# Preparing the queries of the next attention tile one unit ahead, with two sets of query operands

## The chip, the cores and the metric

The kernel runs on one core of a Trainium2 chip. The core has five engines that each work through a queue of their own: TensorE (PE, matrix products and transposes), VectorE (DVE), ScalarE (ACT), GpSimd (POOL) and SyncE (SP), which here issues the transfers. The metric is device time in microseconds of one launch; less is better. Span means the time from the first to the last instruction in one profiled execution.

## The reference

One decoder layer on x of 1024 tokens by 1024 channels, in fp32. Three mixers run side by side on a normed input and a second part is a feed-forward network (FFN):

```
h = rmsnorm(x);  u_pool, q, kv, gates, B, C, X = split(h @ w_in)
y_pool = (window means of 2, 4, 8, 16 tokens - u_pool) @ pool_w * pool_scale    # 256 channels, 4 groups
y_attn = g0 * compressed + g1 * selected + g2 * window                          # 8 heads of 64, 2 key/value groups
y_conv = B * causal_dwconv3(C * X)                                              # 256 channels
x = x + concat(y_pool, y_attn, y_conv) @ w_out
h = rmsnorm(x);  a, g = split(h @ ffn_up)
x = x + (silu(causal_dwconv3(a)) * g) @ ffn_down                                # 2816 hidden units
```

The attention has three branches for each query. The compressed branch looks at 63 compressed keys (blocks of 32 tokens, stride 16). Its probabilities, added up by blocks of 64 tokens, choose the 8 blocks that the selected branch looks at. The window branch looks at the last 512 tokens. Each branch is a softmax with a linear bias by distance and a gate.

## The kernel before

Every fp32 product that needs its precision is made of three products of two parts: an operand is split into `hi` (L88 or L476, ACT) and the rest `lo` (L89 or L477, POOL or DVE), and hi·hi, hi·lo and lo·hi are added up in PSUM.

The program text only states the work. A list scheduler with a simulated timeline sets the order of the instructions on each engine, taking as priority the order in which the text emits them; so an instruction that the text emits later may stand earlier on its engine, and a changed order of emission moves much else. Buffers are rings: a tile with a tag waits until the ring's oldest holder was read for the last time.

The stages, in order of the text:
- First norm, products with `w_in`, compressed keys and values, queries. The queries go to DRAM (`qd`).
- Attention of tiles 0 to 3 of 128 tokens (`attend`, L639), and beside it, as filling work through two PSUM banks (`fill`), the short convolution and the two pooling halves (`pool_half`). A pooling half is: products of normed rows with 128 columns of `w_in` for two halves of the tokens (L211 to L213), copies to `hb` tiles (L694), window sums by doubling on DVE (L712), the scaling and subtraction on DVE (L719 to L721; the first half of the tokens has edge columns of its own), a product with the block-diagonal matrix `bdw` (L723), and a scaled copy on ACT (L725) that goes to DRAM.
- Attention of tiles 4 to 7, and beside it: the output product of the pooling and convolution channels for all tiles (`project`, L820 to L823), then for tiles 0 to 3 the output product of the attention channels, the second norm (`second_norm`: L171 scales, L97 flips, L180 and L181 split into `h2a`), all `up` products of the FFN for these tokens (L841 to L843), and the first three pairs of chunks of the second FFN product for them (L916 and L917; their hidden units, read back from DRAM, are split into `yh` and `yl`, two buffers each). At its end stands the output product of tiles 4 to 7.
- The rest of the FFN (L960), with PE alone to set the pace.

The attention of one tile i is four units: for the two groups g, the window branch (br 1) and the selected one (br 0). A unit has `scores`: per head products into S (L572, L573, masks L576 and L578), maximum (L580, DVE), exponential (L583, ACT), reciprocal (L586, DVE) and gating (L588, POOL). The `values` of the unit before are woven between: transposes of the probabilities (L97), their split (`pth` L476 ACT, `ptl` L477 DVE), products with the values (L609, L610), and after the selected branch the sum of two halves into `yf` (L621).

Ahead of its units a tile needs two functions. `prepare(i)` loads the queries `qn`, transposes them and makes the two operands `qA` (ring) and `qB` (fixed buffers `qB[g][i % QBUF]`, whose constant rows are written once). `compressed(i)` makes the compressed scores (L508 to L510), their softmax in `pc` (L512 maximum, L514 subtraction, L515 exponential, L517 sum, L519 reciprocal, L522 product), for tiles 4 to 7 the choice of blocks (L529 to L541, ending in `pen`, whose transpose goes to rows 96 to 111 of qB), the gating of pc (L549, POOL) and the transposes and split of pc that the values of the first unit read.

With QBUF = 1 the operands of tile i+1 overwrite those of tile i, and `attend` emits `prepare(i+1)` and `compressed(i+1)` after the last unit's scores:

```
            if u and u[1:] == (1, 0) and u[0] < tiles[-1]:
                prepare(u[0] + 1)
                compressed(u[0] + 1)
```

It starts with both for its first tile, so for tile 0 and again for tile 4.

Of the kernel before, what the change touches and what calls it, by code (L numbers as in the profile page):

```python
# [11 lines left out]
I32 = mybir.dt.int32  # L12
# [18 lines left out]
QBUF = 1  # L31

# columns of w_in
# [12 lines left out]
def kernel(  # L46
# [15 lines left out]
    # ------------------------------------------------------------------ pools  # L62
# [11 lines left out]
    def small(w, tag="s8", parts=P, bufs=None):  # L74
        return sm.tile([parts, w], F32, tag=tag, bufs=bufs, name=nm(tag))
# [10 lines left out]
    def split(hi, lo, src, lo_eng):  # L86
        """src = hi + lo exactly, both of at most 12 significant bits"""
        act.activation(hi, src, AF.Copy)  # L88
        lo_eng.tensor_tensor(lo, src, hi.bitcast(F32), ALU.subtract)  # L89

    # -------------------------------------------------------------- constants
# [3 lines left out]
    def flip(out, src, n=P):  # L95
        """transpose of n rows"""
        pe.transpose(out, src, ident[:n, :n])  # L97
# [3 lines left out]
    # rows laid on partitions by one transpose: ffn_conv 66, sconv 6, pool_scale 2, cmp_pos 32  # L101
# [3 lines left out]
    # DRAM scratch  # L105
# [3 lines left out]
    # x with the products of the mixers, then of the attention too  # L109
# [3 lines left out]
    # long-lived attention operands  # L113
# [11 lines left out]
    # values of the compressed branch: rows of the other group are zero  # L125
# [3 lines left out]
    # ---------------------------------------------------------- phase 1 setup  # L129
    pht = ExitStack()  # L130
    hp = pht.enter_context(tc.tile_pool(name="ht", bufs=1, side="right"))
    # normed rows, transposed: two halves of the tokens, each in two parts
# [24 lines left out]
    def rstd_of(ssq, width, n, parts=P, pre=""):  # L157
        """(ssq / n + eps) ** -0.5"""
# [6 lines left out]
    def norm_transpose(xt, g_bc, dst_hi, dst_lo, i, new, bank, pre=""):  # L165
        """RMSNorm of rows xt, transposed and split into dst[:, :, tile i]"""
# [16 lines left out]
    # ------------------------------------------------------------ w_in chunks  # L183
    def load_w(c0, lo_engs, gates=None):
        """256 columns of w_in, and 12 of its gate columns"""
# [11 lines left out]
    def load_w2(src, c0, c1, lo_engs):  # L197
        """two blocks of 128 columns"""
# [7 lines left out]
    def mm_ct(ps, wh, wl, sub, hv):  # L206
        """[channel, token] product of 128 columns with 512 tokens"""
# [7 lines left out]
    def mm_tc(ps, wh, wl, i, n=256):  # L215
        """[token, column] product of tile i with n columns"""
# [7 lines left out]
    def put_gates(ps, i, j):  # L224
        """sigmoid of 12 gate columns"""
# [6 lines left out]
    def head_norm(src, nh, gain, dst, parts=P):  # L232
        """RMSNorm over the 64 columns of each of nh heads; src in PSUM"""
# [11 lines left out]
    def put_v(src, i, br):  # L245
        """split the values [token, 2 groups x 64] of tile i into vv"""
# [5 lines left out]
    # ------------------------------------- first norm, keys and values (selected)  # L252
# [763 lines left out]
```

## Time and profile before

| | |
|---|---|
| Time, three runs | 1353.71, 1354.81 and 1356.84 us; median 1354.81 |
| Profiled execution | span 1351.4 us; what lies around the span is 3.4 us if this execution took the median |
| Busy, share of the span | PE 97%, DVE 56%, ACT 40%, POOL 37% |
| Granted clock of PE | 0.991 in the mean |

The page cuts the span into 40 slices of 33.8 us and gives the busy share in tenths, and the granted clock of PE in the same way:

```profile
PE   6999999999998999999999999999999999999998
...
PEclk9999998989998999999999999999999999999999
```

The slices with an 8 in one of the two rows stand at 203 to 236, 270 to 304 and 405 to 439 us, beside the first slice (start of the program) and the last. The windows in the section on the rows lie around them. In a window's row each engine has its busy time and, in brackets, its number of instructions; PEclk is the granted clock, 1.00 being full. An engine's idle time in a timeline stands in square brackets, with the instruction that ended it.

### The profile page before, as it was taken

How to read it: one execution, taken by the hardware profiler on the slowest of the kernel's cores; microseconds unless marked ns; L12 is line 12 of the kernel's file. 1: busy time of each engine (PE TensorE's matmuls, PEld its weight loads, DVE VectorE, ACT ScalarE, POOL GpSimd, SP SyncE). 2: the span in 40 equal slices, each digit the busy share in tenths (PEclk: the TensorE clock that was granted, in tenths of full speed). 3: DMA queues.
4: the chain of work that ended last, by engine and by line, in shares of the span. 5: the costliest groups of instructions: out<-in, count | busy, mean ns of one | idle time of the engine just before them, and what ended most of it. 6: DMA issues, size and time to landing. Idle time of an engine off the chain costs nothing.

```text
span 1351.4 us, 17763 instructions
## 1 busy us (share of the span) xinstructions
PE 1316.0 (97%) x6670; PEld 1083.8 (80%) x6670; DVE 752.6 (56%) x1351; ACT 536.6 (40%) x972; POOL 496.1 (37%) x447
## 2 busy tenths in 40 slices
PE   6999999999998999999999999999999999999998
PEld 5999987867776788888888878788888888888886
DVE  6762555566677545545654657674454555454554
ACT  5441433445355545444544454452312322132220
POOL 3453722242142544345443454353313331242220
PEclk9999998989998999999999999999999999999999
DMA  9011320145432322222222344231212422243221
GB/s 272 25 42 55 99 75 25 48 147 157 148 125 86 117 87 86 78 87 79 85 89 75 102 136 177 94 120 57 88 59 82 125 63 78 78 156 92 89 70 62
DMA packets 142498, 128.93 MB, mean 95 GB/s; under 512 B 10595, under 2 KB 119373, under 8 KB 142413
## 3 DMA queue, kind: packets, MB, share of 16 engines
q1 hardware_dynamic: 142269, 127.71, 29.9%
q8 instruction: 52, 0.85, 0.3%
q14 instruction: 33, 0.27, 0.1%
q10 hardware_dynamic: 144, 0.10, 0.0%
HBM read 105.50 MB, written 22.28 MB: 95 GB/s over the span
## 4 chain that ended last, share of the span: by engine, by line
PE 88%; DVE 5%; ACT 2%; DMA 2%; issue 1%; POOL 0%; SPq 0%; ACTq 0%; DVEq 0%
PE dn L960 13%; PE fill L841 9%; PE fill L843 9%; PE fill L842 9%; PE tr L97 5%; PE upg L841 3%; PE upg L843 3%; PE upg L842 3%; PE fill L916 3%; PE S L572 2%; PE fill L211 2%; PE fill L213 2%; PE fill L212 2%; PE S L573 2%; PE acc L609 2%; PE acc L610 2%
## 5 line engine op out<-in xcount | busy, mean ns | idle before, releaser
L89 POOL TENSOR_TENSOR wlo<-wst,whi 128x1024 fp32r<-128x1024 f32 x109 | 266.1, 2458 | 282.5 <-ACT whi L88 281.8
L588 POOL TENSOR_SCALAR pb<-pb,rc,gat 128x640 f32<-128x640 f32 (+7 forms) x128 | 105.9, 829 | 315.2 <-DVE rc L586 290.2
L88 ACT ACTIVATE whi<-wst 128x1024 fp32r<-128x1024 f32 x124 | 127.1, 1055 | 116.7 <-DMA wst<-in_ffn_up_dram 76.9
L963 DVE TENSOR_TENSOR x<-dn,x 128x1024 f32<-128x1024 f32 x72 | 88.0, 1222 | 103.8 <-PE dn L960 103.4
L841 PE MATMUL fill<-h2a_hi,whi 128*128 128x512 f32 x352 | 141.8, 403 | 0.5 <-DVE h2a_lo L181 0.5
L843 PE MATMUL fill<-h2a_hi,wlo 128*128 128x512 f32 x352 | 141.6, 402 | 0.0
L842 PE MATMUL fill<-h2a_lo,whi 128*128 128x512 f32 x352 | 141.6, 402 | 0.0
L583 ACT ACTIVATE pb<-S,mx 128x640 f32<-128x640 f32 (+7 forms) x128 | 89.6, 701 | 122.8 <-DVE mx L580 113.6
L477 DVE TENSOR_TENSOR ptl<-tr,pth 128x512 fp32r<-128x512 f32 x140 | 94.3, 686 | 64.7 <-ACT pth L476 32.7
L580 DVE TENSOR_REDUCE mx<-S 128x1 f32<-128x640 f32 (+7 forms) x128 | 89.6, 703 | 67.0 <-PE S L578 65.8
L476 ACT ACTIVATE pth<-tr 128x512 fp32r<-128x512 f32 x140 | 80.4, 596 | 79.1 <-PE tr L97 45.8
L960 PE MATMUL dn<-dl,hh 128*128 128x512 f32 x288 | 89.1, 390 | 0.0
L960 PE MATMUL dn<-dh,hh 128*128 128x512 f32 x288 | 88.6, 391 | 0.3 <-DVE x L963 0.3
L960 PE MATMUL dn<-dh,hl 128*128 128x512 f32 x288 | 88.8, 390 | 0.0
L97 PE MATMUL tr<-ident,pb 128*128 128x128 f32 x528 | 86.0, 276 | 1.1 <-POOL pb L588 1.1
L97 PEld LDWEIGHTS tr<-ident,pb 128*128 128x128 f32 x528 | 65.6, 142 | 15.1 <-POOL pb L588 1.6
L841 PEld LDWEIGHTS fill<-h2a_hi,whi 128*128 128x128 f32 x352 | 66.4, 189 | 14.1 <-DVE h2a_lo L181 0.8
L842 PEld LDWEIGHTS fill<-h2a_lo,whi 128*128 128x128 f32 x352 | 66.4, 189 | 13.5
L843 PEld LDWEIGHTS fill<-h2a_hi,wlo 128*128 128x128 f32 x352 | 66.3, 188 | 13.5
L848 DVE SCALAR_TENSOR_TENSOR f2k<-fill,colw,f2k 128x511 f32<-128x511 f32 x44 | 32.9, 748 | 79.3 <-ACT f2k L847 78.7
L572 PE MATMUL S<-blk,qA 128*128 128x320 f32 (+5 forms) x192 | 71.2, 371 | 5.8 <-ACT pb L583 5.7
L841 PE MATMUL upg<-h2b_hi,whi 128*128 128x512 f32 x176 | 69.2, 394 | 1.8 <-ACT whi L88 1.8
(275 smaller groups left out, 3123.2 us busy)
## 6 DMA issues: line engine op xcount, KB each, us to landing
wst<-in_ffn_up_dram SPq DMA_DIRECT2D x88, 512.0 KB, 3.7
wst<-in_ffn_down_dram SPq DMA_DIRECT2D x28, 512.0 KB, 3.6
wst<-in_w_in_dram SPq DMA_DIRECT2D x18, 512.0 KB, 4.5
wst<-in_w_out_dram SPq DMA_DIRECT2D x12, 512.0 KB, 3.9
hid<-f2k SPq DMA_DIRECT2D x22, 256.0 KB, 2.0
f2k<-hid SPq DMA_DIRECT2D x22, 256.0 KB, 4.2
b<-in_x_dram SPq DMA_DIRECT2D x8, 512.0 KB, 7.2
f<-in_x_dram SPq DMA_DIRECT2D x8, 512.0 KB, 3.4
```

The lines of the kernel that those rows point to most:

```text
L88: act.activation(hi, src, AF.Copy)
L89: lo_eng.tensor_tensor(lo, src, hi.bitcast(F32), ALU.subtract)
L97: pe.transpose(out, src, ident[:n, :n])
L477: dve.tensor_tensor(lo, pt, hi.bitcast(F32), ALU.subtract)
L572: pe.matmul(S[:, c, :cw], qAs[i, g][:, hh, :], kA[br, g][:, cols], start=True, stop=False)
L580: dve.tensor_reduce(mx, S[:, 0:nck, :cw], axis=AX.XY, op=ALU.max, negate=True)
L583: act.activation(pb[:, : ns * P].rearrange("p (c n) -> p c n", c=nck), S[:, 0:nck, :cw], AF.Exp, bias=mx, accum_out=sw)
L588: pool.tensor_scalar(pb[:, : ns * P], pb[:, : ns * P], rc, gat[:, i, col : col + 1], ALU.mult, ALU.mult)
L841: pe.matmul(ps, wh[:, kt, cols], h2[0][:, kt, :], start=kt == 0, stop=False)
L842: pe.matmul(ps, wh[:, kt, cols], h2[1][:, kt, :], start=False, stop=False)
L843: pe.matmul(ps, wl[:, kt, cols], h2[0][:, kt, :], start=False, stop=kt == KT - 1)
L960: pe.matmul(ps[:, nh - turn[0], :], h[:, tt], w[:, nh * 512 : nh * 512 + 512], start=k == 0 and h is hh and w is dh, stop=k == n - 1 and h ...
```

## The change

QBUF becomes 2: a second pair of qB buffers and two buffers for qA of each group. `compressed` is cut in two; `compressed_out` has the gating and the transposes of pc. `attend` emits the three for tile i+1 after three different units of tile i: `prepare` after the scores of (i, 0, 0), `compressed` after those of (i, 1, 1), `compressed_out` after those of (i, 1, 0). This holds across the border from tile 3 to tile 4 too, and only tile 0 has them at the front.

The second set takes room, so that other rings shrink: `qn` and `pc` share one buffer, `yb` moves into the ring of `pth`, `f2k` has 4 buffers instead of 5, `pg` 1 instead of 2, and five tags of small tiles 2 instead of 4. Comments and document strings are taken out too. Lines after the change have numbers 2 to 13 higher.

```diff
-QBUF = 1
+QBUF = 2
...
     def small(w, tag="s8", parts=P, bufs=None):
+        if tag in ("ssq4", "ms4", "rs4", "gate", "cbias"):
+            bufs = 2
...
-    auxq_i = at2.tile([P, P], I32, tag="qn", name="auxq_i")
-    auxq = at2.tile([P, P], F32, tag="qn", name="auxq")
+    auxq_i = at2.tile([P, P], I32, tag="pth", name="auxq_i")
+    auxq = at2.tile([P, P], F32, tag="qn", bufs=1, name="auxq")
...
-        qn = at2.tile([P, 512], F32, tag="qn", name=nm("qn"))
+        qn = at2.tile([P, 512], F32, tag="qn", bufs=1, name=nm("qn"))
...
-        pc = at2.tile([P, 8, 64], F32, tag="pc", bufs=1, name=nm("pc"))
+        pc = at2.tile([P, 8, 64], F32, tag="qn", bufs=1, name=nm("pc"))
...
-                pg = small(64, "pg", bufs=2)
+                pg = small(64, "pg", bufs=1)
...
+        pcg[i] = pc
+
+    def compressed_out(i):
+
+        pc = pcg[i]
         pc4 = pc.rearrange("p (h g) n -> p g h n", g=2)
...
-        yb = at2.tile([64, 4, P], F32, tag="yb", bufs=1, name=nm("yb"))
+        yb = at2.tile([P, 4, P], F32, tag="pth", name=nm("yb"))[0:64]
...
     def attend(tiles):
-        prepare(tiles[0])
-        compressed(tiles[0])
+        if tiles[0] == 0:
+            prepare(0)
+            compressed(0)
+            compressed_out(0)
...
-            if u and u[1:] == (1, 0) and u[0] < tiles[-1]:
-                prepare(u[0] + 1)
-                compressed(u[0] + 1)
+
+            if u and u[0] < NT - 1:
+                if u[1:] == (0, 0):
+                    prepare(u[0] + 1)
+                elif u[1:] == (1, 1):
+                    compressed(u[0] + 1)
+                elif u[1:] == (1, 0):
+                    compressed_out(u[0] + 1)
             prev = (u, pbs)
...
-        return f2.tile([P, 512], dt, tag="f2k", bufs=5, name=nm("f2k"))
+        return f2.tile([P, 512], dt, tag="f2k", bufs=4, name=nm("f2k"))
```

The scheduler's order then differs on every engine from the attention on. Three places follow, each before and after; in the rows a name has its buffer's number behind it.

DVE around the first pooling half, before: the last window sum, the last scaled sums and what comes behind them (`mx` with `tr` is the maximum of the compressed branch of tile 1).

```order
L712 TENSOR_TENSOR hb_3952<-hb_3950 64x525
L721 SCALAR_TENSOR_TENSOR hb_3932<-hb_3950,inv_w,hb_3932 64x512
L586 RECIPROCAL rc_470_2521<-sw_469_2519 128x1
L721 SCALAR_TENSOR_TENSOR hb_3932<-hb_3952,inv_w,hb_3932 64x512
L512 TENSOR_REDUCE mx_454_2479<-tr_2461 128x8
L580 TENSOR_REDUCE mx_472_2528<-S_2524 128x1
L580 TENSOR_REDUCE mx_480_2551<-S_2547 128x1
L514 TENSOR_TENSOR pc_2481<-tr_2461,mx_454_2479 128x512
L517 TENSOR_REDUCE sw_456_2484<-pc_2481 128x8
L519 RECIPROCAL rc_457_2486<-sw_456_2484 128x8
L522 TENSOR_TENSOR pc_2481<-pc_2481,rc_457_2486 128x512
```

DVE there after the change: the start of the same half, from the compressed maximum to the compressed sum.

```order
L514 TENSOR_REDUCE mx_430_2429<-tr_2411 128x8
L586 TENSOR_REDUCE mx_423_2398<-S_2394 128x1
L516 TENSOR_TENSOR pc_2431<-tr_2411,mx_430_2429 128x512
L725 TENSOR_TENSOR hb_4041<-hb_4010 128x527
L592 RECIPROCAL rc_426_2403<-sw_425_2401 128x1
L586 TENSOR_REDUCE mx_435_2443<-S_2439 128x1
L586 TENSOR_REDUCE mx_440_2455<-S_2451 128x1
L725 TENSOR_TENSOR hb_4043<-hb_4041 64x525
L732 TENSOR_TENSOR hb_4041<-hb_4041,inv_c 64x16
L734 SCALAR_TENSOR_TENSOR hb_4010<-hb_4041,inv_w,hb_4010 64x496
L519 TENSOR_REDUCE sw_432_2434<-pc_2431 128x8
```

The compressed branch has moved from behind the half to ahead of it and into it; its reciprocal and product (L521, L524) follow further on, before the second window sums.

DVE at the start of the second pooling half, before: the maximum of a head, then four window sums in a row.

```order
L580 TENSOR_REDUCE mx_602_2908<-S_2904 128x1
L712 TENSOR_TENSOR hb_4197<-hb_4166 128x527
L712 TENSOR_TENSOR hb_4199<-hb_4197 128x525
L712 TENSOR_TENSOR hb_4201<-hb_4199 128x521
L712 TENSOR_TENSOR hb_4203<-hb_4201 64x513
L719 TENSOR_TENSOR hb_4201<-hb_4201,inv_c 64x16
L721 SCALAR_TENSOR_TENSOR hb_4166<-hb_4201,inv_w,hb_4166 64x496
L477 TENSOR_TENSOR ptl_2843<-tr_2837,pth_2842 128x512
L719 TENSOR_TENSOR hb_4203<-hb_4203,inv_c 64x16
```

DVE there after the change, from the first window sum on.

```order
L725 TENSOR_TENSOR hb_4303<-hb_4272 128x527
L479 TENSOR_TENSOR ptl_3103<-tr_3097,pth_3102 128x512
L725 TENSOR_TENSOR hb_4305<-hb_4303 128x525
L725 TENSOR_TENSOR hb_4307<-hb_4305 128x521
L514 TENSOR_REDUCE mx_674_3143<-tr_3125 128x8
L725 TENSOR_TENSOR hb_4309<-hb_4307 64x513
L732 TENSOR_TENSOR hb_4307<-hb_4307,inv_c 64x16
L734 SCALAR_TENSOR_TENSOR hb_4272<-hb_4307,inv_w,hb_4272 64x496
L586 TENSOR_REDUCE mx_679_3157<-S_3153 128x1
L516 TENSOR_TENSOR pc_3145<-tr_3125,mx_674_3143 128x512
L586 TENSOR_REDUCE mx_685_3172<-S_3168 128x1
```

The compressed branch of tile 3 stands between the window sums and scalings now; its sum, reciprocal and product follow some ten rows on.

PE near the end of the early second FFN product, before: a few products L916 with attention work among them (`acc` are the value products of tile 7).

```order
L916 MATMUL fill_8915<-whi_8837,yh_8839 128x512
L916 MATMUL fill_8915<-wlo_8838,yh_8839 128x512
L609 MATMUL acc_6436<-pth_6480,vv 128x512
L916 MATMUL fill_8915<-whi_8837,yl_8840 128x512
L916 MATMUL fill_8915<-whi_8837,yh_8849 128x512
L916 MATMUL fill_8915<-wlo_8838,yh_8849 128x512
L916 MATMUL fill_8915<-whi_8837,yl_8850 128x512
L610 MATMUL acc_6436<-ptl_6481,vv 128x512
L609 MATMUL acc_6436<-pth_6505,vv 128x512
L97 MATMUL tr_6536<-ident,pb_6430 128x128
```

PE after the change, at the border of the second and the third pair of chunks: the next pair has other buffers of `yh` and of the weights.

```order
L929 MATMUL fill_8927<-whi_8849,yl_8852 128x512
L929 MATMUL fill_8927<-whi_8849,yh_8861 128x512
L929 MATMUL fill_8927<-wlo_8850,yh_8861 128x512
L929 MATMUL fill_8927<-whi_8849,yl_8862 128x512
L616 MATMUL acc_6448<-ptl_6620,vv 128x512
L615 MATMUL acc_6448<-pth_6630,vv 128x512
L616 MATMUL acc_6448<-ptl_6631,vv 128x512
L929 MATMUL fill_8957<-whi_8935,yh_8937 128x512
L929 MATMUL fill_8957<-wlo_8936,yh_8937 128x512
```

Three value products stand at this border, and at the one before it three transposes; from the third pair's end to the output product of tiles 4 to 7 no other work is left in the order.

## Rows read from the trace of the kernel before

**Rows 1.** The page: span and instructions, then busy time of each engine.
```profile
span 1351.4 us, 17763 instructions
...
PE 1316.0 (97%) x6670; PEld 1083.8 (80%) x6670; DVE 752.6 (56%) x1351; ACT 536.6 (40%) x972; POOL 496.1 (37%) x447
```

**Rows 2.** Windows: stretch, its length, busy time of each engine, granted clock, DMA.
```profile
193.00:214.88 21.88, 21.88 (x122) 18.35 (x120) 8.08 (x26) 7.97 (x27) 4.73 (x11) 1.00 0.14 44
214.88:227.83 12.95, 10.87 (x49) 8.12 (x47) 10.97 (x29) 5.47 (x17) 4.76 (x7) 0.69 0.08 20
...
290.60:312.20 21.60, 16.86 (x79) 11.03 (x77) 17.29 (x35) 13.94 (x31) 10.17 (x9) 0.84 0.63 218
...
390.97:397.94 6.97, 5.61 (x30) 3.60 (x28) 5.72 (x13) 5.82 (x14) 3.36 (x4) 1.00 0.64 212
397.94:447.37 49.43, 43.16 (x234) 34.75 (x233) 34.91 (x78) 28.00 (x56) 18.33 (x17) 0.93 0.27 91
447.37:800.00 352.63, 352.63 (x1781) 286.77 (x1782) 187.66 (x370) 166.58 (x288) 152.88 (x98) 1.00 0.28 86
```

**Rows 3.** List of waits of PE: total us, times, longest.
```profile
PE S L572 <- ACT pb L583: 5.7, 6, 2.1
...
PE fill L916 <- DVE x L917: 0.6, 1, 0.6
```

**Rows 4.** Timeline of DVE, first pooling half: start us, us, engine, line, operation.
```profile
219.73 0.42 DVE L499 TENSOR_TENSOR qA<-tr,qA 64x256 fp32r<-64x256 f32 x1
...
221.10 0.42 DVE L580 TENSOR_REDUCE mx<-S 128x1 f32<-128x256 f32 x1 [0.41 <-PE S L578]
...
225.93 0.75 DVE L721 SCALAR_TENSOR_TENSOR hb<-hb,inv_w,hb 64x512 f32<-64x512 f32 x1
226.72 0.69 DVE L512 TENSOR_REDUCE mx<-tr 128x8 f32<-128x512 f32 x1
```

**Rows 5.** Timeline of all engines, second pooling half.
```profile
287.27 2.91 DVE L712 TENSOR_TENSOR hb<-hb 128x527 f32<-128x527 f32 x4
...
290.21 0.17 DVE L719 TENSOR_TENSOR hb<-hb,inv_c 64x16 f32<-64x16 f32 x1
...
291.70 4.67 POOL L89 TENSOR_TENSOR wlo<-wst,whi 128x1024 fp32r<-128x1024 f32 x2 [4.29 <-ACT whi L88]
...
293.57 0.69 DVE L477 TENSOR_TENSOR ptl<-tr,pth 128x512 fp32r<-128x512 f32 x1 [2.56 <-ACT pth L476]
...
294.30 2.11 DVE L719 TENSOR_TENSOR hb<-hb,inv_c 64x16 f32<-64x16 f32 x1
...
300.73 0.16 DVE L586 RECIPROCAL rc<-sw 128x1 f32<-128x1 f32 x1 [0.75 <-ACT pb L583]
...
302.20 0.56 DVE L580 TENSOR_REDUCE mx<-S 128x1 f32<-128x384 f32 x1 [0.71 <-PE S L578]
...
303.29 0.84 DVE L621 TENSOR_TENSOR yf<-acc,yb 64x256 f32<-64x256 f32 x2
```

**Rows 6.** Timeline of PE: flips of normed rows, first product of the FFN.
```profile
397.94 1.10 PE L97 MATMUL fill<-ident,f 128*128 128x128 f32 x8
...
411.15 1.09 PE L97 MATMUL fill<-ident,f 128*128 128x128 f32 x8 [0.70 <-DVE f L171]
...
429.95 1.74 PE L97 MATMUL fill<-ident,f 128*128 128x128 f32 x8
...
445.36 1.04 PE L97 MATMUL fill<-ident,f 128*128 128x128 f32 x8
...
447.37 0.50 PE L841 MATMUL fill<-h2a_hi,whi 128*128 128x512 f32 x1 [0.53 <-DVE h2a_lo L181]
```

**Rows 7.** Chain of waits, a piece of products at full clock.
```profile
905.82 2.99 PE dn L960 x13
```

**Rows 8.** Operations on the tile yh: durations in ns, shortest, median, longest.
```profile
L88 ACT ACTIVATE yh<-f2k x21: 619/632/634, 308.6 to 870.9; 128x512 fp32r<-128x512 f32 x21
...
L89 POOL TENSOR_TENSOR yl<-f2k,yh x10: 1285/1298/1307, 371.4 to 848.2; 128x512 fp32r<-128x512 f32 x10
```

More of the change, by code (lines that the diff above doesn't have):

```diff
@@ L478, in put_pt @@
         return hi, lo
-    qAs, pcs, yfs, pos = {}, {}, {}, {}
+    qAs, pcs, pcg, yfs, pos = {}, {}, {}, {}, {}
     new_s, new_p = [None], [None]
     def prepare(i):
-        qn = at2.tile([P, 512], F32, tag="qn", name=nm("qn"))
+        qn = at2.tile([P, 512], F32, tag="qn", bufs=1, name=nm("qn"))
         nc.sync.dma_start(qn, qd[i])
```

## The prediction

> **What bounds the kernel now.** I read the page first. Its sum of busy times shows TensorE (PE) busy for 1316.0 of 1351.4 us, every other engine at 56% or less [rows 1]. So a change of order can win only what PE does not use: pauses, and stretches in which its clock is low. The windows come second, laid along the attention, because the change touches nothing after it but buffer counts. They show that this loss stands in few places [rows 2]. In the 352.63 us from 447.37 to 800.00, which hold most of the boundaries between tiles 4 to 7, PE works 352.63 us at full clock: preparing the next tile later or earlier is worth nothing there. From 193.00 to 214.88 it is the same, 21.88 of 21.88 us. The loss stands in four windows: the second part of the first pooling half (214.88 to 227.83, pause 12.95 − 10.87 = 2.08 us, clock 0.69), that of the second (290.60 to 312.20, 4.74 us, 0.84), the run-up to the second norm (390.97 to 397.94, 1.36 us) and the second norm of tiles 0 to 3 (397.94 to 447.37, 6.27 us, 0.93). The pauses add up to 14.45 us; the low clock costs at most 12.95 × 0.31 + 21.60 × 0.16 + 49.43 × 0.07 = 10.9 us. All that could be won is 25.4 us at the most.
>
> The list of waits comes third. PE's own waits for the attention's softmax chain are small, S behind the previous head's exponential 5.7 us in six [rows 3], so the waits the change aims at are short. What VectorE (DVE) has queued in the four windows decides, and I read its timeline there.
>
> **First pooling half.** The DVE work of this half (L712 to L721) fills the window from its start to 226.68, mixed with softmax work of tiles 0 and 1; the compressed branch of tile 1 (its 128x512 operations take 0.69 us each) comes behind it, from 226.72 on [rows 4]. PE has little else until the two small products with bdw have the pooled channels. In the new order (shown above) the compressed maximum and subtraction stand ahead of the first window sum, and the sum, the reciprocal, the product and two yf additions inside it: 0.69 + 0.16 + 0.69 + 0.84 = 2.4 us (the reciprocal by the nearest row, the two yf in one row) [rows 4, 5]. Counted between the first window sum and the last scaled one, three maxima more (0.42 each) and two reciprocals more (0.16) add 1.6, and the two qA subtractions leave (0.42 each, −0.8): +3.2 us. The two operations ahead, 2 × 0.69 = 1.4 us, may run while PE still has its input product, so they cost 0 to 1.4; I take 0.8, near the middle. The window grows by 4.0 us; PE has three more heads of scores in it, some 1.0 us of its own work by their count at the pace of [rows 7], which is then missing later. **Term: +3.0 us**, bounds 0 (all of it falls into DVE's own pauses there) and +4.
>
> **Second pooling half.** Here DVE idles before: 2.56 us ahead of 293.57, and 0.7 us twice, all for ScalarE or PE; and one 64x16 product takes 2.11 us where the same one took 0.17 [rows 5]. POOL then runs two weight splits, from 291.70 to 296.37. The Trainium skill, "SBUF — State Buffer", section "SBUF: two separate sides", states that a DVE operation with two SBUF inputs and a GpSimd operation that reads SBUF lock one port pair for a whole instruction and the other waits fully. The trace agrees: the small product ended with the second of POOL's operations. By that rule the new order, which keeps such sums and splits side by side and puts more into this queue, pays at least once more; without it the second half would come out 2.3 us cheaper than I have it.
>
> By the rows: in the old order the four window sums begin at 287.27, 3.3 us before the window, in the new one some 0.5 us before it, since the queue now reaches them later: +2.8. Five operations of tile 3's compressed branch move in (4 × 0.69 + 0.16 = +2.9) and fill the pauses, 2.56 + 0.75 + 0.71 = −4.0. The 1.94 us that the small product lost goes, and I put one new collision at half of POOL's pair, 4.67 / 2 = 2.34. Sum +2.1; PE has about 1.0 us more to do in it. **Term: +1.1 us**, bounds −1.2 (no collision) and +5.1 (the pauses stay, because they wait for ScalarE and not for DVE work).
>
> **Run-up and second norm.** From the first flips of a normed tile (397.94) to the first product of the FFN (447.37) four cycles stand: 13.21, 18.80, 15.41 and 2.01 us [rows 6]. The first is plain; the second holds the choice of blocks for tile 4. In the new order that of tile 5 stands between the third and fourth flips instead, so that I expect 13.2 + 13.2 + 18.8 + 3.0 = 48.2, 1.2 less. Counted in the order at PE's pace (0.23 us for a 512 wide product, [rows 7]), the attention work between these two marks grows from about 36.2 to 40.4 us. If the cycles are bound by the chain (square, rsqrt, scaling, flips, split), the extra 4.2 us fall into the 6.27 us of pause and are won; if PE bounds them, they are not. 1.2 to 5.4, and I take the middle. **Term: −3.5 us**, bounds 0 and −9.7 (pause and low clock gone). In the run-up 2.1 us less PE work is left behind the last mixers' product, which takes most of its pause. **Term: −1.0**, bounds −1.4 and 0.
>
> **The end of the attention.** All attention now ends earlier, by some 22 us of PE work in the order. In the old order it is mixed with the early part of the second FFN product (L916) and hides the changes of pair there: PE's whole wait for them is 0.6 us [rows 3]. In the new one three transposes (0.3 us) and three value products (0.7 us) are left for two changes and nothing for the third, to the projection. The hidden units of a pair use yh and yl, two buffers each: the new chunk's ScalarE copy (0.63) and POOL split (1.30) [rows 8] can begin when the old pair's first chunk has done its last product, three products (0.7 us) before the pair's end. 0.63 + 1.30 − 0.7 is 1.2, less the cover 0.9 and 0.5, and 0.7 for the third: 2.1 us. **Term: +1.4**, bounds 0 and +3.
>
> **Costed at nothing.** Two more memsets and eight small scalings for the second qB run while PE is full [rows 2]. qn and pc in one buffer: the query load of a tile waits for the flips of the previous pc, a unit and more before the operands are used, covered by that unit's scores; if the cover failed, a load and two flips would show as a PE wait at L97 in every tile. Four f2k buffers for five: the hidden units are loaded through SP's queue behind the up weights, in the same order as before; a failure would show as pauses in the FFN. The smaller pools of tiny tiles add waits of POOL only in the query norms, where PE is full.
>
> **Sum.** 3.0 + 1.1 − 3.5 − 1.0 + 1.4 = +1.0. Span 1351.4 + 1.0 = 1352.4; the median 1354.81 is 3.4 us above the profiled span, so 1355.8 us: no change that can be told from none, about 0.2% (2.7 us) being what a measurement can tell.
>
> **Rivals.**
> (a) Faster: the norm stage is chain-bound and the added attention work takes all its pauses and keeps the clock up. −9.7 − 1.4, second half −1.2, first half 0, end +1.4: −10.9, 1343.9 us. For it: PE pauses and clock falls just there. Against it: those pauses come in the cycle with the choice of blocks, which stays. Chance 0.23.
> (b) Slower: the pooling chain is the bound of its windows, DVE works it off in order, and the compressed branch in front delays the small products, so the clock falls longer. From the point at which DVE has no pause left in the window it pays in full. +3.0 + 5.1, nothing won in the norm stage, end +1.4: +9.5, 1364.3 us. For it: DVE is busy 10.97 of 12.95 us in the first window. Against: 4 us of DVE pause in the second. Chance 0.24.
> (c) It only moves work earlier and PE stays the bound: all terms nought, 1354.8. Chance 0.08.
> (d) The Trainium skill, "Perfetto Trace Analysis", section "Identifying Performance Opportunities", reads gaps that repeat on the engine that should be full as a sign of too few buffers. The mechanism would be that the single set of query operands makes every pause in the attention; a second set would then win back the whole 25.4 us, 1329.4. The rows speak against it, since tile boundaries from 447.37 on show no pause at all with one set. Chance 0.04.
> The forecast has 0.41, with its own range 1352 to 1360.
>
> **Numbers.** Faster by over 0.2% (under 1352.1): (a), (d) and a little of the forecast, 0.28. Within: most of the forecast, (c) and edges of (a) and (b), 0.36. Slower (over 1357.5): (b) and the upper part of the forecast, 0.36. The range reaches to 1343 and 1365, (a) and (b) nearly whole.
>
> **What would show it.** First half: the compressed sum and product between window sums on DVE, and the window from the last input product to the next longer than 12.95 us. Second half: a 64x16 product or a window sum of 2 us beside a POOL split. Norm: one cycle of about 18.8, now the third, and less than 6.27 us of pause. End: PE waits at the three changes of pair. I am wrong if the pauses of the pooling windows shrink, if new pauses show between 447 and 800, or if the FFN after 910 is longer.

## The result, and the profile after

The changed kernel takes 1372.91 us (median of four, 1370.11 to 1374.6) against 1354.88; the ratio is 1.0129 with a 95% interval of 1.0115 to 1.0142. By the ratio it is slower by 17.5 us (the medians lie 18.0 us apart); 1355.8, no change, was forecast, and 1365 was the end of the range. The likeliest was wrong, and the rival that came nearest is (b), slower, though its place was only one of several.

The page after: span and instructions, busy time of each engine, granted clock in 40 slices.

```profile
span 1368.4 us, 17852 instructions
...
PE 1319.8 (96%) x6670; PEld 1084.1 (79%) x6670; DVE 767.3 (56%) x1359; ACT 534.2 (39%) x972; POOL 495.2 (36%) x449
...
PEclk9999999998999999999999999999999999999999
```

PE has 3.8 us more of busy time than before [rows 1] in a span 17.0 us longer: the work is the same, and what grew is pauses, with some work at the low clock. The windows after stand at the same marks of the program as those before, to within one product of PE; the first is the first pooling half, then the second half to its last product with bdw, the run-up, the second norm, the `up` products, and the early second FFN product.

```profile
216.06:230.84 14.78, 10.90 (x51) 7.43 (x50) 13.45 (x35) 7.98 (x25) 5.90 (x9) 0.77 0.13 35
301.90:328.86 26.96, 18.21 (x85) 12.20 (x84) 26.47 (x46) 12.82 (x28) 14.29 (x11) 0.87 0.53 177
411.26:416.44 5.18, 3.87 (x23) 2.52 (x21) 3.85 (x9) 3.24 (x7) 2.73 (x3) 1.00 0.92 268
416.44:472.77 56.33, 48.66 (x266) 39.03 (x267) 43.30 (x86) 32.68 (x67) 23.77 (x22) 0.94 0.27 83
472.77:831.00 358.23, 358.23 (x1797) 289.76 (x1797) 187.50 (x348) 167.67 (x285) 151.98 (x97) 1.00 0.28 86
831.00:881.75 50.75, 46.86 (x215) 36.91 (x213) 29.73 (x44) 16.78 (x27) 19.55 (x12) 0.97 0.53 184
```

The early second FFN product before, and the output product of tiles 4 to 7 behind it:

```profile
803.37:863.33 59.96, 59.40 (x305) 47.39 (x304) 41.02 (x66) 29.85 (x51) 28.85 (x20) 1.00 0.45 158
863.33:893.05 29.72, 29.72 (x136) 24.01 (x135) 23.29 (x29) 15.32 (x23) 11.32 (x8) 1.00 0.27 89
```

The norm stage takes 56.33 us instead of 49.43 [rows 2], its pause is 7.67 us instead of 6.27; the early second FFN product has 3.89 us of pause where it had 0.56, and DVE is busy for 26.47 of 26.96 us in the second pooling half. The run-up holds 1.74 us less work of PE (3.87 us, 5.61 before), but its pause is 1.31 us as it was 1.36. The `up` products have none, before and after: the forecast that nothing is to be won there held.

Windows of different length hide how much work lies in them, because the new order moves attention work across the marks. So I count each stage as the time on PE less what its instructions take at pace (for each kind of instruction the 30th percentile of the distance to the next start, from the trace of before). What is left is the stage's loss, pauses and low clock together, and the losses add up to the difference of the spans (98.2 − 81.3, which is 17.0 us before rounding). In the table the stages are A, B (first and second pooling half, B with the first projections behind it), the run-up (here all that lies between B and C, which is more than its window above), C (second norm), D (early second FFN product, L916 before and L929 after), E (output product of tiles 4 to 7 and their norm) and the rest.

```
us of loss                    A     B   run-up  C     D     E    rest   sum    ratio, 95% interval
before                       7.3  11.0   6.0  12.6   3.1   1.4  39.9   81.3   1
after                        8.7  16.4   7.6  15.2   7.2   3.8  39.4   98.2   1.0129 [1.0115, 1.0142]
early place, one thing changed
  e3 only queries ahead      9.3  17.8   7.7   9.8   7.6   4.0  41.9   98.1   1.0104 [1.0084, 1.0125]
  e4 no crossing             8.9  16.8  11.4  18.7   3.2   3.9  41.9  104.9   1.0154 [1.0129, 1.0178]
  e5 POOL splits in pieces   9.8  16.0   7.0  10.7   1.7   4.0  37.3   86.4   1.0070 [1.0053, 1.0087]
  e6 last split on POOL      8.6  14.8   7.4  14.6   3.0   3.9  37.9   90.3   1.0080 [1.0065, 1.0095]
  e8 tile 3 compressed late  8.8  16.0   9.0  15.1   3.7   3.8  38.1   94.5   1.0092 [1.0077, 1.0107]
  e9 tile 5 choice late      8.9  13.0   7.5  11.5   8.6   3.9  38.6   92.0   1.0095 [1.0080, 1.0110]
  e10 three places right     8.9  16.1   9.1  13.1   3.6   2.5  39.8   93.1   1.0069 [1.0047, 1.0090]
  e11 tile 3 all late        8.7  15.6   9.7  12.1   7.1   3.4  39.5   96.0   1.0113 [1.0087, 1.0140]
old place
  e1 rings only, one set     7.6  13.9   5.5  14.2   2.8   6.4  43.0   93.3   1.0083 [1.0056, 1.0110]
  e2 rings and two sets      9.3  11.0   4.1  16.2   3.7   2.9  38.6   85.8   1.0027 [1.0015, 1.0039]
  r1 qn and pc one buffer    7.9  15.2   7.2  13.5   3.3   1.5  41.8   90.3   1.0061 [1.0041, 1.0081]
  r2 yb in the pth ring      7.3  11.0   3.6  15.3   3.5   5.8  39.6   86.1   1.0043 [1.0030, 1.0056]
  r3 one pg                  7.1  11.4   5.9  13.6   5.2   5.3  41.4   90.0   1.0045 [1.0027, 1.0063]
  n5 heads in other order    8.2  12.7   5.9  11.5   2.5   9.3  42.1   92.2   1.0090 [1.0065, 1.0115]
  e5b before, in pieces      6.7  18.1   4.3  18.3   4.2   1.0  40.6   93.1   1.0066 [1.0042, 1.0090]
  e13 e2, in pieces          6.1  14.1   6.8  15.0   2.9   5.3  38.4   88.6   1.0036 [1.0025, 1.0046]
```

The losses come from one profiled execution each, and that limits them. On PE, DVE, ACT and POOL the kernels e4, e6 and e9 have the order of after up to the end of B, and B is 16.8, 14.8 and 13.0 there beside 16.4; r3 has the order of before up to C, and B is 11.4 beside 11.0. So B lost between 1.6 and 5.8 us, and one trace does not say where in between. A, the run-up and C repeat better: 8.6 to 8.9 for A, 7.4 to 7.6 for the run-up (e6, e9), 14.6 and 15.2 for C (e6) in the order of after, 7.1 and 7.3 for A in that of before (r3). The ratio is the measurement.

PE's list of waits after has three single ones that were small before or missing (those for pen, for pc and for x):

```profile
PE tr L99 <- DVE pen L543: 5.5, 1, 5.5
PE S L578 <- ACT pb L589: 5.2, 10, 1.6
PE tr L99 <- DVE pc L516: 4.4, 1, 4.4
PE fill L929 <- DVE x L930: 3.9, 1, 3.9
```

Before, the wait for pc was not there, that for x was 0.6 us [rows 3], and that for pen:

```profile
PE tr L97 <- DVE pen L541: 1.5, 1, 1.5
```

The wait for S, which the change was to shorten, is 5.2 us; it was 5.7 [rows 3].

**Second norm.** The flips of the four normed tiles and the first product of the FFN after:

```profile
416.44 1.09 PE L99 MATMUL fill<-ident,f 128*128 128x128 f32 x8
...
430.28 1.03 PE L99 MATMUL fill<-ident,f 128*128 128x128 f32 x8
...
444.38 1.04 PE L99 MATMUL fill<-ident,f 128*128 128x128 f32 x8
...
468.67 1.15 PE L99 MATMUL fill<-ident,f 128*128 128x128 f32 x8
...
472.77 0.47 PE L854 MATMUL fill<-h2a_hi,whi 128*128 128x512 f32 x1
```

The cycles are 13.84, 14.10, 24.29 and 4.10 us long; the third holds the choice of blocks of tile 5, as forecast, and is 5.5 us longer than forecast. All engines, where PE waits for pen:

```profile
455.04 4.68 POOL L91 TENSOR_TENSOR wlo<-wst,whi 128x1024 fp32r<-128x1024 f32 x2
...
455.36 2.09 DVE L535 SCALAR_TENSOR_TENSOR imp<-pg,imp 128x16 f32<-128x16 f32 x1
...
457.48 2.27 DVE L536 SCALAR_TENSOR_TENSOR imp<-pg,imp 128x15 f32<-128x15 f32 x1
...
462.03 0.15 DVE L535 SCALAR_TENSOR_TENSOR imp<-pg,imp 128x16 f32<-128x16 f32 x1
...
462.35 0.17 DVE L536 SCALAR_TENSOR_TENSOR imp<-pg,imp 128x15 f32<-128x15 f32 x1
...
462.66 0.38 PE L99 MATMUL tr<-ident,pen 128*16 128x128 f32 x1 [5.49 <-DVE pen L543]
```

Two operations on 16 columns take 2.09 and 2.27 us while POOL runs two weight splits, and end with one split each; the same two operations for the other group take 0.15 and 0.17 us at 462.03 and 462.35. This is what the product at 294.30 showed in the second pooling half [rows 5]. The Trainium skill, "SBUF — State Buffer", section "SBUF: two separate sides", gives the rule (two SBUF inputs on DVE against a GpSimd operation that reads SBUF: the later one waits for the whole instruction), and these rows agree.

**Second pooling half.** All engines again:

```profile
303.01 3.49 DVE L725 TENSOR_TENSOR hb<-hb 128x525 f32<-128x525 f32 x2
...
303.06 5.64 POOL L91 TENSOR_TENSOR wlo<-wst,whi 128x1024 fp32r<-128x1024 f32 x2
...
306.42 0.68 DVE L514 TENSOR_REDUCE mx<-tr 128x8 f32<-128x512 f32 x1
...
307.13 2.12 DVE L725 TENSOR_TENSOR hb<-hb 64x513 f32<-64x513 f32 x1
...
310.49 0.67 DVE L516 TENSOR_TENSOR pc<-tr,mx 128x512 f32<-128x512 f32 x1
...
311.31 0.63 PE L99 MATMUL tr<-ident,pb 128*128 128x128 f32 x4 [4.36 <-DVE pc L516]
```

Three window sums take 5.6 us beside two splits, 3.5 more than three times the 0.69 that one takes (at 301.72), and the compressed maximum and subtraction stand between and behind them in DVE's queue. PE waits 4.36 us for the subtraction, because the transposes of probabilities take their PSUM banks from the same three `tr` banks that the compressed scores still hold.

**Early second FFN product.**

```profile
866.76 2.36 POOL L91 TENSOR_TENSOR wlo<-wst,whi 128x1024 fp32r<-128x1024 f32 x1
...
866.85 3.35 DVE L91 TENSOR_TENSOR wlo<-wst,whi 128x1024 fp32r<-128x1024 f32 x1 [1.74 <-POOL yl L91]
...
870.99 1.29 DVE L930 TENSOR_TENSOR x<-fill,x 128x512 f32<-128x512 f32 x2
...
871.74 0.80 PE L929 MATMUL fill<-whi,yh 128*128 128x512 f32 x1 [3.89 <-DVE x L930]
```

A weight split on DVE for the last output product takes 3.35 us beside POOL's, and the sum that frees PE's PSUM bank is behind it. Before, a split on DVE met POOL's too, at 865.12: it took 2.89 us for half the columns, and the weight split behind it, alone, 1.21.

```profile
865.06 2.40 POOL L89 TENSOR_TENSOR wlo<-wst,whi 128x1024 fp32r<-128x1024 f32 x1 [11.05 <-ACT whi L88]
865.12 2.89 DVE L89 TENSOR_TENSOR yl<-f2k,yh 128x512 fp32r<-128x512 f32 x1
...
867.94 1.21 DVE L89 TENSOR_TENSOR wlo<-wst,whi 128x1024 fp32r<-128x1024 f32 x1
```

PE had attention work and the output product under way and did not wait. The cover is gone now, since the attention ends earlier (last score product 847.83 before, 842.60 after, while L916 and L929 begin at 803.37 and 831.45).

### The profile page after: what moved, and what is told of

Read it like the earlier page. It is cut to its first block, busy times and chain, and to the rows that moved or that the text cites. A ratio compares the mean times of both kernels' runs of the same rounds, so it can differ in the third digit from the quotient of the medians.

```text
span 1368.4 us, 17852 instructions
## 1 busy us (share of the span) xinstructions
PE 1319.8 (96%) x6670; PEld 1084.1 (79%) x6670; DVE 767.3 (56%) x1359; ACT 534.2 (39%) x972; POOL 495.2 (36%) x449
## 4 chain that ended last, share of the span: by engine, by line
PE 77%; DVE 3%; issue 2%; DMA 2%; ACT 2%; POOL 1%; ACTq 0%; SPq 0%; POOLq 0%; DVEq 0%
PE dn L973 13%; PE fill L854 9%; PE fill L856 9%; PE fill L855 9%; PE tr L99 4%; PE upg L854 3%; PE upg L856 3%; PE upg L855 3%; PE S L578 2%; PE S L579 2%; PE acc L616 2%; PE acc L615 2%; PE fill L213 2%; PE fill L214 2%; PE fill L215 2%
## 5 line engine op out<-in xcount | busy, mean ns | idle before, releaser
L976 DVE TENSOR_TENSOR x<-dn,x 128x1024 f32<-128x1024 f32 x72 | 87.9, 1221 | 100.6 <-PE dn L973 100.6
```

## Experiments

**Which part of the change?** Theory P was the early place, S the smaller rings, N the order as such. e1 is before with the rings of the change; e2 to e4 are after with another place of emission:

```diff
 e2, and e4 with the early places left inside a call
+        prepare(tiles[0]); compressed(tiles[0]); compressed_out(tiles[0])
-        if tiles[0] == 0: ...
 e2
+            if u and u[1:] == (1, 0) and u[0] < tiles[-1]:
+                prepare(u[0] + 1); compressed(u[0] + 1); compressed_out(u[0] + 1)
 e4
-            if u and u[0] < NT - 1:
+            if u and u[0] < tiles[-1]:
 e3
-                elif u[1:] == (1, 1): compressed(u[0] + 1)
+                elif u[1:] == (1, 0): compressed(u[0] + 1); compressed_out(u[0] + 1)
```

> The kernel before with one set of query operands and its old places, but with the smaller rings of the change (qn and pc share a buffer, yb in the ring of pth, 4 f2k, 1 pg, 2 of five small tags). Theory P (the place: the compressed branch and the choice of blocks now stand in the middle of a tile, on VectorE beside POOL's weight splits, and PE waits behind them): 1352 to 1359 us, the choice of blocks costs PE under 3 us and the second pooling half is left within 24 us. Rival S (the smaller rings make the new waits): 1368 to 1375 us. Rival N (any edit shakes up the scheduler's order, and the time with it): anything from 1350 to 1375.

> The changed kernel with two sets and smaller rings, but preparation, compressed branch and gating emitted at the old place, after the last unit's scores, and for tile 4 at the start of its call. P: back to 1352 to 1359 us, since the place is undone. S: 1368 to 1375, since the rings stay small. N: anything from 1350 to 1375.

> The changed kernel with the queries prepared early, after unit (i,0,0), but the compressed branch, the choice of blocks and the gating together after the last unit's scores. P: most of the loss goes, 1353 to 1361 us, for the part moved early is only transposes and copies. S: 1368 to 1375. N: anything from 1350 to 1375.

> The changed kernel without the step across the border: tile 4 is prepared at the start of its own call, the rest stays early. P: the loss in the second pooling half stays (it holds tile 3's compressed branch), in the second norm the order changes so that its share may go or stay: 1360 to 1372 us. S: 1368 to 1375. N: anything from 1350 to 1375.

Measured: 1365.97, 1359.32, 1369.21 and 1375.95 us against 1354.88. No theory holds alone. The old place takes back most of the loss (e2, 1.0027) and all of that in B; but the same rings at the same place with one set cost 1.0083, and the crossing left out makes it worse (1.0154) although it undoes a part. P fails on e1 and e3, S on e2; e1 lies between the ranges of P and S, and e4 just above all three. N's range of 1350 to 1375 holds e1 to e3, but says little. Between e1 and e2 only the second set differs, and it is 0.56% faster: whether that is the set or the order it brings is not shown.

**The lock, and one split.** In e5 every weight split on POOL is cut into pieces; e6 puts the last output product's splits on POOL alone:

```diff
 e5, e5b, e13: in split()
-        lo_eng.tensor_tensor(lo, src, hi.bitcast(F32), ALU.subtract)
+        n = 1
+        if lo_eng is pool:
+            n = min(4, lo.shape[1]) if len(lo.shape) == 3 else max(1, lo.shape[1] // 256)
+        for k in range(n):
+            r = slice(k * lo.shape[1] // n, (k + 1) * lo.shape[1] // n)
+            lo_eng.tensor_tensor(lo[:, r], src[:, r], hi[:, r].bitcast(F32), ALU.subtract)
 e6
-    ws = load_wout((2, 4), (pool, dve))
+    ws = load_wout((2, 4), (pool, pool))
```

> The changed kernel with every weight split on POOL cut into pieces of 256 columns a partition (512 for w_out), so that one POOL instruction is 0.6 to 1.2 us long instead of 2.4. Theory L (VectorE operations with two SBUF inputs stand still until POOL's running instruction ends): the slow ones beside POOL (2.1 and 2.3 us for the 16 wide operations of the choice of blocks, 2 us more on the window sums) come to under 1.3 us each, PE's wait for pen from 5.5 to under 3, time 1362 to 1368 us. Rival (the waits are the length of the chain, the lock only lies beside it): PE's wait for pen stays over 4.5, 1370 to 1376 us.

> The changed kernel with all weight splits of the last output product (tiles 4 to 7) on POOL instead of half of them on VectorE; the order is the same up to that product. L: the 3.35 us split on VectorE beside POOL's, behind which the sums of L930 stand, is gone, and with it PE's wait of 3.9 us in the early second FFN product: 1367 to 1370 us. Rival: POOL becomes late for the output product instead and PE waits there, 1371 to 1375 us.

Measured: 1361.4 and 1363.45 us, against 1352.24 there; the expectations were made from 1354.88, so the ratios are to be compared. In e6 the stage D falls from 7.2 to 3.0 us, to that of before. All engines in e6 at the place:

```profile
864.22 4.73 POOL L91 TENSOR_TENSOR wlo<-wst,whi 128x1024 fp32r<-128x1024 f32 x2
...
865.76 1.29 DVE L930 TENSOR_TENSOR x<-fill,x 128x512 f32<-128x512 f32 x2
...
866.50 0.50 PE L929 MATMUL fill<-whi,yh 128*128 128x512 f32 x1 [1.19 <-DVE x L930]
```

The sums now come beside POOL's split in their usual time (one input is in PSUM), and PE waits 1.19 us instead of 3.89. This is the one place where cause and price are shown with the order unchanged up to the edit: the split that stands on DVE ahead of the sums costs 4.2 us in D. How much of that is the lock (3.35 us instead of 1.21) and how much the split itself, e6 does not separate. The ratio fell further than forecast, to 1.0080 (1367 to 1370 us are 1.0089 to 1.0112), and 1.6 us of it stand in B, where the order is the same. e5 falls in the range of theory L, from 1.0129 to 1.0070 (1362 to 1368 us are 1.0053 to 1.0097), with C 4.5 and D 5.5 us shorter. Its order is another one, though: the choice of blocks does not stand beside a split in it, the wait for pen is not in PE's list, and that for S is 10.9 us instead of 5.2. So it supports the lock and does not prove its price. The same pieces made before slower (e5b) and did not help e2 (e13), against theory L in both; e13 falls in the range of its rival, e5b lies above both:

> The kernel before with POOL's weight splits in pieces of 256 columns. L: the 2.11 us product of the second pooling half and the 2.17 us one of the choice of blocks come under 1.3 us; PE's loss falls by 1 to 4 us, ratio 0.997 to 0.999. Rival: 0.9995 to 1.005, since the order moves and POOL has more instructions.

> Two sets and smaller rings with the old place of everything, and POOL's weight splits in pieces of 256 columns. P and L together: the run with the old place alone was at 1.0027; the pieces take what is left of the 2 us waits in the second pooling half and the norm stage: 0.997 to 1.001. Rival: the pieces cost POOL's own time per instruction and shift the order, 1.002 to 1.008.

1364.5 and 1359.37 us against 1354.24. In e5b PE waits 9.6 us for the edge columns of the second pooling half (`PE fill L728 <- DVE hb L725: 9.8, 2, 9.6`), a wait that before does not have.

**Tiles 3 and 5 put back.** e8 and e9 emit the compressed branch of one tile late, e11 all of tile 3's preparation, and e10 is e6, e8 and e9 together:

```diff
 e8 with (2,), e9 with (4,), e10 with (2, 4)
-                elif u[1:] == (1, 1):
+                elif u[1:] == (1, 0 if u[0] in (2,) else 1):
                     compressed(u[0] + 1)
-                elif u[1:] == (1, 0):
+                if u[1:] == (1, 0):
                     compressed_out(u[0] + 1)
```

> The changed kernel with the compressed branch of tile 3 alone at the old place, after the last unit's scores of tile 2; the order is the same up to the second pooling half. P (the place makes the waits): PE's wait of 4.4 us for the compressed subtraction goes, the loss of the second pooling half falls by 3 to 5 us to that of before, 1366 to 1370 us, if what comes behind it stays. Rival (the pooling chain itself is late there, whatever stands in it): the loss stays, 1371 to 1376 us.

> The changed kernel with the compressed branch and choice of blocks of tile 5 alone at the old place; the order is the same up to the second norm. P: PE's wait for pen (5.5 us) moves behind the first up products, where other work fills it, the norm stage falls by 3 to 5 us, 1367 to 1370 us. Rival: the norm's own chain (sums, scale, flips, split) is the bound there and its loss stays, 1371 to 1376 us.

> The changed kernel with the queries, the compressed branch and the gating of tile 3 all at the old place; the order is the same until shortly before the second pooling half. Where only the compressed branch was put back the loss of this half stayed (16.0 us over PE's pace, 11.0 before). Theory Q (the early queries let tile 3's attention run ahead, so that its softmax meets the pooling chain): the loss of the half falls to 10 to 13 us, time ratio 1.005 to 1.009. Rival (the half is set by what ran before it: tiles 1 and 2 early too, so PE has too little attention left for it): the loss stays at 15 to 17, ratio 1.010 to 1.015.

> The changed kernel with the compressed branch of tiles 3 and 5 at the old place and the last output product's weights split on POOL alone. If the parts add up: 4.2 us from the early second FFN product and 3.7 from the second norm, 0 to 2 from the second pooling half: ratio 1.005 to 1.008. If the scheduler's order takes back elsewhere what a part gives: 1.008 to 1.013.

Measured: 1365.35 and 1365.98 (1352.24 there), 1369.51 (1354.24) and 1362.45 us (1352.25). In e9 the wait for pen is gone, and C falls from 15.2 to 11.5 us, 1.1 under that of before; but D is 8.6. Its ratio, 1.0095, is in the range of P (1367 to 1370 us are 1.0089 to 1.0112). PE's waits in e9:

```profile
PE tr L99 <- DVE pc L516: 4.4, 1, 4.4
PE fill L929 <- DVE x L930: 3.8, 3, 3.1
```

In e8 the wait for the compressed subtraction is gone too, but B stays at 16.0: PE waits for the yf sums in its place, which stand in the same queue of DVE. Its ratio of 1.0092 is in the range of P (1366 to 1370 us are 1.0082 to 1.0112), but by luck: what fell is D (3.7 us), not B.

```profile
PE tr L99 <- DVE pen L543: 5.5, 1, 5.5
PE acc L605 <- DVE yf L627: 4.3, 3, 2.6
```

With all of tile 3 late (e11) B is still 15.6, and e10, with e8's order there, has 16.1; the order of after gave 13.0 to 16.8. So no fall of B is seen without tile 3's compressed branch, and that step of theory P fell. e10 comes to 1.0069, the best of the repaired versions beside e5, in the range forecast for the sum of its parts; in its trace D is 3.6 us shorter than after and C 2.1, where 4.2 and 3.7 were counted.

**Is it the order as such?** r1 to r3 are before with one ring of the change each, and n5 is before with the heads of the compressed scores emitted in the order 0, 4, 1, 5, ..., no buffer changed:

```diff
 n5
-            g, hh = divmod(h, 4)
+            hh, g = divmod(h, 2)
```

> The kernel before with one ring changed: queries and compressed probabilities share one buffer (and the integer constants move to the ring of pth). S (this ring makes the wait that cost 11 us with all the smaller rings and one set): the query load waits for the previous tile's probabilities at every tile, PE waits at the transposes of qn, ratio 1.005 to 1.009. N (no wait of its own, only another order): no PE wait at qn in the profile, and a ratio anywhere from 0.997 to 1.006.

> The kernel before with yb in the ring of pth alone. S: the split of probabilities waits for the sums of yf, PE waits at the value products in the tiles after that, ratio 1.002 to 1.006. N: a ratio anywhere from 0.998 to 1.008, its loss in the pooling half or the norm.

> The kernel before with one buffer for pg instead of two; the order is the same up to the second norm. S: the second group's sum of the choice of blocks waits for the first group's, the norm stage is 1 to 4 us longer, ratio 1.001 to 1.003. N: 0.998 to 1.006, by whichever stage the order reaches.

> The kernel before, with the heads of the compressed scores emitted in the order of PSUM columns instead of group by group: no buffer, no place and no amount of work changes, but the scheduler's order does from there on. Theory N (this kernel's order is a favourable one, and most others cost some tenths of a per cent): ratio 1.003 to 1.009, with longer losses in the pooling halves or the norm and no wait for a buffer. Theory S (lack of room is what costs): 0.998 to 1.002.

Measured: 1362.74 us (1354.24 there), 1358.87, 1359.69 and 1364.33 (1352.25). r1 has no wait at the transposes of qn among PE's waits; new is 1.1 us at the compressed scores for the split of qA, too little for 8 us, and it stands in n5 too, where no ring was changed:

```profile
PE S L572 <- ACT pb L583: 6.0, 7, 2.0
...
PE tr L508 <- DVE qA L499: 1.1, 1, 1.1
...
PE tr L97 <- DVE pen L541: 0.2, 1, 0.2
```

n5 changes no buffer, so nothing could run short, and it costs 0.9%. Most of its loss is in E, not in the pooling halves or the norm, where it was expected: the attention ends late there. The output product of tiles 4 to 7 begins at 861.59 (865.05 before) and the last value product of tile 7 at 890.43 (878.16 before), so that PE, with the last tile's product next, waits for its split:

```profile
861.59 0.47 PE L820 MATMUL fill<-whi,yh 128*128 128x512 f32 x1
...
890.43 0.50 PE L610 MATMUL acc<-ptl,vv 128*128 128x512 f32 x1 [0.22 <-DVE ptl L477]
...
893.15 0.50 PE L820 MATMUL fill<-whi,yh 128*128 128x512 f32 x1 [2.23 <-ACT yh L88]
```

The same wait of 2.2 us stands in the lists of e1 and r2; before does not have it. So theory N stands best: six kernels at the old place, with none of the early steps and none in pieces (e1, e2, r1 to r3, n5), cost 1.0027 to 1.0090, 1.0058 in the mean, and none reaches the order of before. Only n5 changes the order alone. The others change rings, and that a ring costs them nothing is argued from PE's list of waits; waits on the other engines were not followed. The early place unrepaired (after, e3, e4) costs 1.0104 to 1.0154, 1.0129 in the mean.

## Why the prediction was wrong

By the terms of its sum, forecast and measured loss (after less before):

```
first pooling half    +3.0    +1.4
second pooling half   +1.1    +5.4
run-up                -1.0    +1.6
second norm           -3.5    +2.6
end of the attention  +1.4    +6.5  (D +4.1, E +2.4)
all else               0      -0.5
sum                   +1.0   +17.0
```

- **Second norm** is the step that failed by most, 6.1 us. I had the choice of blocks of tile 5 in the right cycle (between the third and fourth flips, 24.3 us long instead of the 18.8 taken over), but took its length from the norm stage of before, where it met no POOL split. It meets two, which cost DVE 4.0 us, and the next instruction in PE's queue is the transpose of pen, so PE waits 5.5 us instead of 1.5. I had weighed the lock for the second pooling half only. The other half of this term failed too: with the choice out of the way (e9) the stage is 1.1 us better than before and not 3.5, so most of the attention work added there did not fall into its pauses; why is open.
- **End of the attention:** that the cover goes was right, and the price was looked for in the wrong place. Not the yh and yl of the next pair make PE wait, but DVE's own weight split for the output product, next to POOL's (e6). And the output product of tiles 4 to 7 with its norm, now with no attention beside it, loses 2.4 us, which I had at nothing. PE's list shows 0.9 us there for POOL's `wlo` and 1.0 for the sums of L976; that the missing attention is the cause is not shown, for n5 loses more in this stage with attention beside all but its last tile.
- **Second pooling half:** the collisions in DVE's queue that I counted are there, two slow window sums instead of one slow product, and PE waits 4.4 us behind them. But they are not shown to be the price: without tile 3's compressed branch or its queries the loss stays (e8, e10, e11). The 5.4 us are just over the upper bound of 5.1 that rival (b) used, and the same order gave 2.0 to 5.8 in other executions (over the 11.0 of before). What in the order makes it is open; old places have B from 11.0 to 18.1.
- **Run-up:** the 2.1 us less of PE work came (1.74 in the window), and the pause that it should have taken stayed, 1.31 us for 1.36. The run-up of the table, which is longer, even lost 1.6 us more; by what is not shown.
- **First pooling half:** the compressed operations stand where I read them, and the price was half.
- **Costed at nothing:** the rings. None shows a wait of its own in PE's list, as I said, but those of qn and pc, of yb and of pg move the order, and the kernels with one of them cost 0.4 to 0.6% (r1 to r3), that with all of them 0.8% (e1). The fewer f2k buffers and the small tags were not tried alone.
- **Two slips in the sum:** the middle of 1.2 and 5.4 is 3.3 and not 3.5, and 2.1 less the 0.6 of before is 1.5 and not 1.4. Beside misses of 5 us they do not matter.

Of the signs named ahead, the compressed operations among the window sums, window sums of over 2 us beside a POOL split and a long third cycle came. Less than 6.27 us of pause in the norm (7.67) and waits at all three changes of pair (one, of 3.9 us) did not.

Under these lies one error of method. I summed small terms of both signs as if the rest of the order stayed as good as it was. The order before was a favourable one among its neighbours: each of six edits that moved it and left the old places cost 4 to 12 us. How the 17.5 us divide is an estimate, from means over few and related kernels: some 8 us (0.58%) for what another order costs on average, and some 10 (1.0129 less 1.0058) for the early place, of which e6 and e9 show 4.2 and 3.7 in two stages. The direct pair, after against e2 with the same rings and sets, puts 1.02% (14 us) on the early place and the order that it brings. Rival (d), by which a second set wins back 25.4 us, is refuted: e2 has the two sets and is slower than before. Rival (c), all terms nought, falls with the ratio of 1.0129. That rival (b) came nearest is in part luck: it had the pooling halves for its cause, and more than half of the loss stands in the norm and the end of the attention.

## What to carry to other kernels

Where a scheduler sets the order, run a null edit first, one that reorders and changes nothing else: its spread is the least uncertainty of any forecast that sums small terms, and if the present order is better than all its neighbours, the risk is on the slow side. Look at what stands beside a moved chain on the other engines, not at the chain alone: a 16 column operation with two SBUF inputs took 2.3 us beside a POOL split instead of 0.17. Work that is finished earlier is missing later as cover, and what it covered (here a slow split) must be looked for.

## What was not expected of the hardware

Cutting POOL's weight splits from 1024 columns into pieces of 256 (512 for w_out) does not by itself make the kernel faster: with the early place 1.0129 became 1.0070, with the old one 1.0027 became 1.0036 and 1 became 1.0066.

And the same order of instructions lost 16.4, 16.8, 14.8 and 13.0 us in the second pooling half in four executions (after, e4, e6, e9). Between the same two products of PE, after and then e9:

```profile
270.65:348.62 77.97, 69.22 (x337) 52.33 (x335) 53.24 (x103) 36.24 (x82) 28.88 (x28) 0.93 0.36 116
```

```profile
270.55:345.17 74.62, 67.79 (x337) 51.58 (x335) 53.11 (x103) 36.12 (x82) 28.80 (x28) 0.95 0.37 122
```

PE has the same 337 instructions in both; of the 3.35 us between them 1.92 are pauses of PE, and 1.43 are work that took longer at a granted clock of 0.93 instead of 0.95. What makes one execution pause more is open. The two larger losses come from where the kernel before took 1354.88 us, the two smaller from where it took 1352.24.
